# Row softmax on one core: which queue issues the first load, and which load has its last row split

## The chip, the cores and the metric

The kernel runs on one core of a Trainium2 chip. The metric is device time in microseconds (us). Times of several runs are given as their median; the profile is that of one execution.

## What is computed

The input `x` is 16 x 1024 rows of 512 float32 numbers, the output has the same shape:

```python
x_scaled = x / 2.0
x_max = np.max(x_scaled, axis=-1, keepdims=True)
exp_x = np.exp(x_scaled - x_max)
return (exp_x / np.sum(exp_x, axis=-1, keepdims=True)).astype(np.float32)
```

Each row is read once and written once: 33.55 MB in each direction.

## The kernel before, in words

The 16384 rows are 128 rows for each of the 128 partitions. `PLAN` cuts them into ten tiles. Tile 0 has 3 rows a partition, tile 1 has 7, tile 2 has 13, and tiles 3 to 9 have 15 each. Each tile is loaded by one request and stored by one request (with one exception, below), and is worked on in chunks: 1 chunk in tile 0, 2 in tile 1, and 3 in every other tile, of 3 to 5 rows a partition. There are 27 chunks.

All tiles live in one buffer, `arena`, of 98 rows a partition. Tiles 0 to 7 fill it. Tile 8 takes the place of tiles 0 to 2, and tile 9 that of parts of tiles 2 and 3, so their loads have to wait until those tiles are stored (`behind`, `need`). Everything is computed in place.

The engines work on a chunk in this order, with semaphores between them:

- VectorE takes the maximum of each row, negated (`do_max`, L118). The first chunk of a tile waits for the tile's load semaphore `ld[t]`.
- ScalarE computes exp(0.5 x - 0.5 max) row by row, and the same instruction sums the row (L176 for tiles 0 to 5, L211 in a loop for tiles 6 to 9).
- VectorE takes the reciprocal of the sums (L127) and multiplies, in one instruction for a chunk of tiles 1 to 3 (`FUSED`, L131) and row by row elsewhere (L138). It does this two chunks behind the maxima (`LAG` = 2): maximum of chunk k, then reciprocal and product of chunk k - 2.
- SyncE (SP) waits for a tile's last product and issues its store (L158). At the end it waits for the last stores (L162).

Two engines issue loads in `issue_loads`, and each has a DMA queue of its own: SP's is q1 in the profile, ScalarE's is q10. SP issues the load of tile 0 (L105), and later all stores. ScalarE issues all other loads. Tile 1, the tile whose number is `SPREAD`, goes in three requests (L110): its first six rows on all partitions, its last row on partitions 0 to 125, and its last row on partitions 126 and 127. Its first chunk therefore waits for 48 counts of its semaphore instead of 16. The others go whole (L114).

The order in time is written out by hand. `issue_loads(0, 2)` is moved into the program's first block, ahead of the barrier of all engines with which a program starts (L252 and L37 in the profile), so that the loads of tiles 0 and 1 are issued before the engines meet. The loads of tiles 2 to 7 follow behind the barrier, in order, on ScalarE; then ScalarE loads its table of exp (L171). The loads of tiles 8 and 9 stand among its exponentials (L190), behind the last chunk of tiles 4 and 5, each with its wait for the stores that free its place.

Of the kernel before, what the change touches and what calls it, by code (L numbers as in the profile page):

```python
# [14 lines left out]
ARENA = 98  # L15
LAG = 2

SPREAD = 1

AFTER = {8: 4, 9: 5}  # L20

# [7 lines left out]
def kernel(  # L29
# [5 lines left out]
    nc = tc.nc  # L35
# [4 lines left out]
    xf = x.flatten_outer_dims()  # L40
# [24 lines left out]
    def dram(ap, t):  # L65
        b, r, _ = tiles[t]
        return ap[b * P : (b + r) * P].rearrange("(p r) d -> p r d", r=r)

    def sb(t):
        _, r, at = tiles[t]  # L70
        return arena[:, at : at + r, :]
# [9 lines left out]
    ld = [nc.alloc_semaphore(f"ld{t}") for t in range(len(tiles))]  # L81
# [16 lines left out]
    def issue_loads(begin, end):  # L98


        for t in range(begin, end):
            if t in behind:
                continue
            if t == 0:
                nc.sync.dma_start(out=sb(t), in_=dram(xf, t)).then_inc(ld[t], 16)  # L105
            elif t == SPREAD:

                r = tiles[t][1] - 1
                for p, q, lo, hi in ((0, P, 0, r), (0, 126, r, r + 1), (126, P, r, r + 1)):
                    nc.scalar.dma_start(  # L110
                        out=sb(t)[p:q, lo:hi], in_=dram(xf, t)[p:q, lo:hi]
                    ).then_inc(ld[t], 16)
            else:
                nc.scalar.dma_start(out=sb(t), in_=dram(xf, t)).then_inc(ld[t], 16)  # L114

    def do_max(k):
# [5 lines left out]
            negate=True,  # L122
        )._wait_ge(ld[t], 48 if t == SPREAD else 16).then_inc(s_max, 1)

# [102 lines left out]
    entry.instructions = []  # L227
    nc.switch_bb("main", None)
    issue_loads(0, 2)
    first = list(entry.instructions)  # L230
    at = next(k for k, i in enumerate(head) if type(i).__name__ == "InstDrain")
    entry.instructions = head[:at] + first + head[at:]
    act = []
    entry.instructions = list(entry.instructions) + [i for i in jumps if i not in act]
    nc.switch_body(here, parent=None, valid_engines=[i.engine for i in jumps])
    issue_loads(2, len(tiles))
    compute_and_store()

# [29 lines left out]
```

## Time and profile before

| | before |
|---|---|
| median of 10 runs | 160.09 us (160.06 to 160.2) |
| profiled execution, its own time | 160.07 us |
| its span, first to last instruction | 158.7 us |
| busy VectorE, ScalarE | 131.4 us, 94.4 us |
| packets' time on q1 and q10, share of 16 DMA engines | 50.5%, 48.6% |
| first load packet, last store packet's completion | 1.0 us, 158.3 us |
| VectorE's wait for loads | 14.8 us in 5 waits |
| last load landed, last store issued | 127.4 us, 147.2 us |

The span is what the trace covers; the execution's own time has 1.4 us more around it. A page of the profile gives busy times, a strip of 40 slices of the span with the busy share of each engine in tenths, and the DMA queues. "q1" and "q10" are shares of the time of all 16 DMA engines; a tile's load or store is cut into 128 row blocks, one a partition, eight on each engine, and each appears in the trace as a packet with its start, its length and its bytes. Behind the packets of a request, each engine that took part writes a small completion, and these count the semaphore up.

### The profile page before, as it was taken

Reading aid. Unit: us, or ns where it says so; the run is one execution under the profiler, and the core shown is the slowest. Engines: PE = TensorE matmul, PEld = TensorE weight load, DVE = VectorE, ACT = ScalarE, POOL = GpSimd, SP = SyncE. Lnnn points to the kernel's source line nnn. Section 1 sums busy time; section 2 is a strip of 40 time slices with the busy share of each in tenths; the row PEclk is TensorE's granted clock in tenths of the full one; section 3 lists DMA queues with packets and bytes.
Section 4 is the critical chain, followed back from the end, with each engine's and each line's share of the span. In section 5 each row is a group of like instructions: output and inputs, shape, how many; then the busy total and the mean of one; then the engine's idle time right before and its main releaser. Section 6 shows DMA issues by size and latency. Waiting matters only on the chain.

```text
span 158.7 us, 621 instructions
## 1 busy us (share of the span) xinstructions
DVE 131.4 (83%) x155; ACT 94.4 (59%) x257; POOL 0.2 (0%) x4
## 2 busy tenths in 40 slices
DVE  0367699999999999999999999996999379999000
ACT  0359297736964684679638886667566809764000
POOL 0000000000000000000000000000000000000000
DMA  7999999999999999999999999999999999999996
GB/s 262 456 365 429 411 434 460 428 397 436 458 448 401 428 462 451 403 459 403 457 410 457 410 449 418 426 441 418 449 418 449 418 449 418 449 418 441 410 457 263
DMA packets 3026, 67.13 MB, mean 423 GB/s; under 512 B 336, under 2 KB 336, under 8 KB 720
## 3 DMA queue, kind: packets, MB, share of 16 engines
q1 hardware_dynamic: 1584, 34.34, 50.5%
q10 hardware_dynamic: 1440, 32.77, 48.6%
q14 instruction: 2, 0.02, 0.0%
HBM read 33.55 MB, written 33.55 MB: 423 GB/s over the span
## 4 chain that ended last, share of the span: by engine, by line
DMA 52%; DVE 38%; issue 0%
DMA arena<-in_x_dram 38%; DVE stats L118 18%; DMA out_dram<-arena 14%; DVE arena L131 13%; DVE arena L138 7%; DVE recip L127 1%
## 5 line engine op out<-in xcount | busy, mean ns | idle before, releaser
L118 DVE TENSOR_REDUCE stats<-arena 128x5 f32<-128x2560 f32 (+2 forms) x27 | 72.2, 2676 | 14.8 <-DMA arena<-in_x_dram 14.8
L176 ACT ACTIVATE arena<-arena,stats 128x512 f32<-128x512 f32 x68 | 48.2, 710 | 23.7 <-DVE stats L118 23.7
L211 ACT ACTIVATE arena<-arena,stats x60 | 42.5, 710 | 20.5 <-ACTq L203 20.5
L138 DVE TENSOR_SCALAR arena<-arena,recip 128x512 f32<-128x512 f32 x93 | 38.6, 483 | 0.7
L131 DVE TENSOR_TENSOR arena<-arena,recip 128x2560 f32<-128x2560 f32 (+2 forms) x8 | 19.9, 2492 | 0.3
L176 ACT ACTIVATION_READ_ACCUMULATOR arena<-arena,stats 128x1 f32 x68 | 12.7, 187 | 0.0
L211 ACT ACTIVATION_READ_ACCUMULATOR arena<-arena,stats x60 | 11.2, 187 | 0.0
L127 DVE RECIPROCAL recip<-stats 128x5 f32<-128x5 f32 (+2 forms) x27 | 4.8, 178 | 0.0
L171 ACT ACT_TABLE_LOAD x1 | 1.3, 1283 | 5.9 <-issue 5.9
L252 POOL MEMSET const-bfloat16-1.0<- 128x1 bf16 x1 | 0.1, 101 | 0.0
L252 POOL MEMSET const-uint8-127<- 128x1 uint8 x1 | 0.1, 101 | 0.0
L252 POOL MEMSET const-float32-0.0<- 128x1 f32 x1 | 0.1, 98 | 0.2 <-issue 0.2
L252 POOL MEMSET const-float32-1.0<- 128x1 f32 x1 | 0.1, 98 | 0.0
## 6 DMA issues: line engine op xcount, KB each, us to landing
arena<-in_x_dram ACTq DMA_DIRECT2D x7, 3840.0 KB, 46.7
out_dram<-arena SPq DMA_DIRECT2D x7, 3840.0 KB, 22.7
arena<-in_x_dram ACTq DMA_DIRECT2D x1, 3328.0 KB, 14.7
out_dram<-arena SPq DMA_DIRECT2D x1, 3328.0 KB, 20.9
out_dram<-arena SPq DMA_DIRECT2D x1, 1792.0 KB, 17.7
arena<-in_x_dram ACTq DMA_DIRECT2D x1, 1536.0 KB
arena<-in_x_dram SPq DMA_DIRECT2D x1, 768.0 KB, 6.4
out_dram<-arena SPq DMA_DIRECT2D x1, 768.0 KB, 15.7
```

Of the source, the lines that this page charges most:

```text
L118: nc.vector.reduce_max(out=stats[:, b : b + c], in_=arena[:, a : a + c], axis=mybir.AxisListType.X, negate=True,)._wait_ge(ld[t], 48 if t ...
L127: nc.vector.reciprocal(out=recip[:, b : b + c], in_=stats[:, b : b + c])._wait_ge(s_exp, k + 1).then_inc(s_rec, 1)
L131: nc.vector.tensor_mul(out=arena[:, a : a + c], in0=arena[:, a : a + c], in1=recip[:, b : b + c].unsqueeze(2).to_broadcast([P, c, D]),)._w ...
L138: ins = nc.vector.tensor_scalar_mul(out=arena[:, a + r], in0=arena[:, a + r], scalar1=recip[:, b + r : b + r + 1],)
L171: nc.scalar.preload_act_table(mybir.ActivationFunctionType.Exp)
L176: ins = nc.scalar.activation(out=arena[:, a + r], in_=arena[:, a + r], func=mybir.ActivationFunctionType.Exp, bias=stats[:, b + r : b + r ...
L211: ins = nc.scalar.activation(out=data, in_=data, func=mybir.ActivationFunctionType.Exp, bias=stat, scale=0.5, accum_out=stat,)
L252: nc = _bacc.Bacc("TRN2", target_bir_lowering=False, num_devices=1)
```

## The change

`SPREAD` becomes 5, and the branch that gave tile 0 to SP goes:

```diff
-SPREAD = 1
+SPREAD = 5
...
         for t in range(begin, end):
             if t in behind:
                 continue
-            if t == 0:
-                nc.sync.dma_start(out=sb(t), in_=dram(xf, t)).then_inc(ld[t], 16)
-            elif t == SPREAD:
+            if t == SPREAD:
 
                 r = tiles[t][1] - 1
                 for p, q, lo, hi in ((0, P, 0, r), (0, 126, r, r + 1), (126, P, r, r + 1)):
                     nc.scalar.dma_start(
                         out=sb(t)[p:q, lo:hi], in_=dram(xf, t)[p:q, lo:hi]
                     ).then_inc(ld[t], 16)
             else:
                 nc.scalar.dma_start(out=sb(t), in_=dram(xf, t)).then_inc(ld[t], 16)
```

ScalarE now issues tiles 0 and 1, each whole, ahead of the barrier; behind it, it issues tiles 2, 3 and 4 whole, tile 5 in three requests (fourteen rows on all partitions, the last row on partitions 0 to 125, the last row on 126 and 127), and tiles 6 and 7 whole. SP issues stores only. In `do_max`, which is not edited, the count of 48 follows `SPREAD` to tile 5; tile 1's first chunk waits for 16. All shapes of computation, all stores and the loads of tiles 8 and 9 are as before. The line numbers of the profile behind the edit move up by 2.

## The prediction

> **What bounds the kernel now.** I read the page first, then a table by stage, then the DMA view of two stretches at the start, and last the waits.
>
> ```profile
> DVE 131.4 (83%) x155; ACT 94.4 (59%) x257; POOL 0.2 (0%) x4
> ...
> DMA  7999999999999999999999999999999999999996
> ...
> DMA packets 3026, 67.13 MB, mean 423 GB/s; under 512 B 336, under 2 KB 336, under 8 KB 720
> ...
> HBM read 33.55 MB, written 33.55 MB: 423 GB/s over the span
> ```
>
> The DMA line is at 9 in every slice but the first and the last: the 16 DMA engines, not VectorE (83%), are full. Table by stage (stretch, its length, busy DVE, ACT, POOL, clock, DMA share, GB/s):
>
> ```profile
> 0.00:1.00 1.00, 0.00 (x0) 0.00 (x0) 0.20 (x4) 1.00 0.00 0
> 1.00:2.50 1.50, 0.00 (x0) 0.00 (x0) 0.00 (x0) 1.00 0.92 299
> 2.50:6.40 3.90, 0.02 (x1) 0.49 (x1) 0.00 (x0) 1.00 1.03 411
> 6.40:9.70 3.30, 1.76 (x2) 2.33 (x6) 0.00 (x0) 1.00 1.14 407
> ...
> 17.40:59.20 41.80, 41.52 (x25) 27.01 (x75) 0.00 (x0) 1.00 1.01 435
> ...
> 127.90:147.50 19.60, 19.07 (x33) 10.91 (x30) 0.00 (x0) 1.00 1.03 442
> 147.50:157.40 9.90, 0.00 (x0) 0.00 (x0) 0.00 (x0) 1.00 0.96 416
> ```
>
> Nothing moves for 1.0 us; then the engines are full until 157.4, at 299 to 411 GB/s in the first stages and 430 to 442 later. Single packets say the same: the first starts at 1.006 us (SP's load of tile 0, issued at 0.00), a row block of 30720 bytes takes 1.138 us wherever it stands, and the 16 engines write their last completion between 157.43 and 158.26. So the span is first packet + each engine's bytes + what is lost to slow packets, and an edit counts if it changes one of these or lets an engine go empty. VectorE's chain is a second, near bound at the end only: the last load lands at 127.45, VectorE starts on it at 127.85, the last store is issued at 147.17, and its first packet starts at 148.35, directly behind the store before it.
>
> The profiled execution took 160.07 us, 1.37 over its span of 158.7; the median of the ten runs is 160.09. I add differences to 160.09. A measurement of this kernel tells about 0.2% (0.32 us) from no change.
>
> **Part 1: tile 0 moves from SP's queue to the front of ScalarE's.** SP loses one issue of 0.378 us, and nothing else waits there until the first store at 15.04. ScalarE issues tile 0 at L114 where it issued tile 1, at 0.12 us, 0.12 later than SP did. How long ScalarE's first packet takes after its issue is not shown directly:
>
> ```profile
> DMA packets 73, 0.45 MB, mean 179 GB/s; under 512 B 0, under 2 KB 0, under 8 KB 73
> ...
> q1 hardware_dynamic: 73, 0.45, 55.0%
> ```
> ```profile
> q10 hardware_dynamic: 90, 1.11, 81.0%
> q1 hardware_dynamic: 71, 0.34, 23.5%
> ```
>
> The first fence is 0 to 2.5 us, with SP's queue q1 alone; the second 2.5 to 6.0 us, where ScalarE's q10 joins in. Tile 1, issued at 0.12, has its first packet only at 2.52. Is ScalarE's queue late by itself, or had the engines taken SP's packets already? Followed packet by packet, every one of the 16 engines does exactly five packets of q1 (the first 0.23 to 0.73 us, the rest 0.234) before its first of q10, though they began between 1.006 and 1.788 us. One late moment common to all, or one fixed delay, would not give five everywhere: engine by engine they would need windows that don't overlap. So it is a depth to which an engine commits to a queue, and q10's descriptors were there much earlier. The stores show this again: tile 0's store, issued at 15.04, starts at 18.51, behind load packets already taken. Bounds for the shift of the first packet: 0 (issue as early as SP's, same delay of 1.006) to +1.5 (2.52, as if the queue itself were that late). I take ScalarE's 0.12 plus SP's 1.006 = 1.126, a shift of **+0.12 us**, since SP's row is the nearest without another queue ahead. The Trainium skill ("DMA: Bandwidth & Descriptors", "Latency and other measured facts") gives about 0.6 us to the first byte for both issuing engines alike; SP's row has 1.006 - 0.378 = 0.63. By the page ScalarE's first packet would come at 0.12 + 0.385 + 0.6 = 1.1, a shift of 0.1; no row here shows it for ScalarE.
>
> Tiles 0 and 1 no longer share the engines packet by packet. Tile 0 (8 packets an engine, 8 x 0.230 = 1.84 us) lands after about 1.126 + 0.4 (slow first packet) + 1.84 = 3.4 us, on the two engines that start 0.77 later at about 4.2, instead of 6.00. VectorE's first maximum starts near 4.6 instead of 6.38. The 1.8 us are no gain: the next is ScalarE's table load (below) and then tile 1's landing, and the DMA engines stay full throughout.
>
> **Part 2: tile 1 in one piece.** Per engine 8 x 0.531 = 4.25 us, instead of 8 x 0.456 + 9 x 0.080 = 4.37 on fourteen engines and 3.65 on two. Those two are the late starters, 7.84 us at the end of tile 1's wide part against 7.0 to 7.4 for most. Unsplit, all are on tile 2 by about 7.96, where three engines were last at 8.57 to 8.76. Tile 2's last row block ended at 16.91; I expect 16.5, and VectorE's long run from 17.36 starts up to 0.4 earlier. Cost on the end: **0**, as the engines are full and tile 2's store only joins a queue. Without that cover (an engine idle) 0.4 would be a gain, not a loss.
>
> **Part 3: issues around the barrier.** Ahead of the barrier ScalarE issues two DMAs instead of three. Rows of L110: 0.385, 0.665, 0.244. I take 0.385 + 0.5, so L114's later issues begin near 2.2 instead of 2.65 (bounds 2.0 and 2.65). There are then eight issues instead of six: 3.23 + 0.665 + 0.244 = 4.14, ending at 6.3, and the table load of 1.283 ends near 7.6 instead of 7.19. First exponential before: 8.16. So it comes some 0.5 earlier at 7.6, bound by the table load and no longer by VectorE. Tile 2's descriptors come near 3.2 and are needed at 7.1. All of it lies beside full DMA engines: **0**. If that cover were gone, tile 0's store would be late; at 15.04 it has no one waiting for it.
>
> **Part 4: the split in tile 5.** Fourteen engines get 8 packets of 28672 bytes (about 1.06 us each, estimated between the 0.983 of 26624 and 1.134 of 30720 bytes) and nine of 2048 (0.080); two engines get none. Total bytes of every engine are as before, since the row that leaves them sits in another tile: **0** on the last packet. 336 packets under 512 B are 20 x 16 + 14 + 2 completions, and that count stays. What is new is where the small packets run: in tile 1 no other queue was active, while at about 53 us tile 2's store is. There loads and stores alternate one by one in the packets. About four store packets (0.987 each) are left then, so four small loads wait for one each: on most engines tile 5 ends at 53.7 + 0.1 (9 x 0.080 for 8 x 0.074) + 4 x 0.987 = 57.8, and it lands near 58 instead of 55.26. It is wanted by the thirteenth maximum at 64.00: 6 us of cover. Tile 2's store ends 4 us earlier in exchange, then loads run alone until tile 3's store, issued at 59.18 with first packet at 62.73; by then both queues have moved the same bytes as before. The Trainium skill ("DMA: Bandwidth & Descriptors", "Queues, rings and completion order") has an engine drain a packet of typically 9 to 17 descriptors from one ring before it turns to the next. By that the nine small rows would go through together and tile 5 would land near 55.4. The rows contradict it here; both land before 64. If the cover were gone, the maximum would wait 4 us.
>
> **Sum:** +0.12 + 0 + 0 + 0 = +0.12. Slow packets stay, I assume: over their steady lengths they cost, mean per engine, 0.31 us in 1.0 to 2.5, 0.26 in 2.5 to 6.0 and 0.57 in 7.7 to 9.6 (tile 2's first packets take about 1.53 instead of 0.987). I allow -0.06 for less switching between queues. 160.09 + 0.06 = **160.15 us**.
>
> **Rivals.**
>
> *Slower, ScalarE's queue starts late.* For it: the 2.52 above, and no row of ScalarE's queue alone. Against it: five packets everywhere. From 1.39 us for the first packet it adds over 0.32. To have been in turn at the sixth packet, q10 must have been there by the second, at 1.57 at the latest on the engine with the earliest; so the likely price is up to +0.56, 160.65; at 2.52 it is 161.6.
>
> *Slower, the end starves.* The last store is issued at 147.17; with SP's 1.006 it is there at 148.18, and its first packet starts at 148.35: cover of 0.17 us. Tile 9's completions come between 124.76 and 127.44, three engines being one store packet (1.138) behind the others. If the new order puts one more store packet before the last load on the last engine, VectorE ends 1.14 later, and the earlier engines idle for 1.14 - 0.17 = 0.97: from 157.43-157.69 to about 158.4-158.7, over the 158.26 of the latest. Price +0.15 to +0.4: 160.25 to 160.5. Against it: tile 2 lands earlier, and loads run ahead around 60 us.
>
> *Faster, slow packets go.* If the slow stretches after 2.5 us come from two queues or from small rows, 0.26 + 0.57 = 0.83 go: 160.21 - 0.83 = 159.4; the stretch at 7.7 alone: 159.64. Against it: the two engines without small rows are slowed as much (1.53 and 1.57).
>
> *Nothing changes:* the sum, with the shift anywhere near zero.
>
> **Chances.** Forecast 0.45, all within 0.2% (159.77 to 160.41). Late queue 0.25, slower. Starved end 0.12, a third of it within 0.2%. Slow packets gone 0.18, faster. Faster 0.18, same 0.45 + 0.04 = 0.49, slower 0.25 + 0.08 = 0.33. The range is 159.6 to 160.7: below it lies the loss of both slow stretches (about 0.1), above it a queue later than 1.6 us (about 0.1).
>
> **What will show it.** Right: first load packet at 1.1 on q10, no q1 packet before the first store; tile 0's maximum near 4.6, first exponential near 7.6; VectorE's run from about 17.0 to 17.4; tile 5 landing near 58 without an idle VectorE at the thirteenth maximum; last store's first packet directly behind the store before it; last completion near 158.3. Wrong: a first packet after 1.4, an idle gap in q1 near 148, or 430 GB/s already before 9 us.

## The result and the profile after

The changed kernel takes 160.60 us (median of 8 runs, 160.55 to 160.89) against 160.09 (28 runs, 159.98 to 160.23). The ratio is 1.0036, 95% interval 1.0027 to 1.0044: slower by about half a microsecond. The profiled execution took 160.86 us with a span of 159.5, at the upper end of its runs. So the two profiled executions lie 0.79 us apart where the medians lie 0.51 apart, and the details below show more loss than the medians do.

The page of the changed kernel, the lines that answer to those of before:

```profile
DVE 131.5 (82%) x155; ACT 94.3 (59%) x257; POOL 0.2 (0%) x4
...
DMA  6999999999999999999999999999999999989888
...
DMA packets 3026, 67.13 MB, mean 421 GB/s; under 512 B 336, under 2 KB 336, under 8 KB 720
...
HBM read 33.55 MB, written 33.55 MB: 421 GB/s over the span
```

Work, bytes and packets are the same to the unit. New is the end of the DMA strip: 8s where there were 9s. The same table by stage as before (stretch, length, busy DVE, ACT, POOL, clock, DMA share, GB/s):

```profile
1.00:2.50 1.50, 0.00 (x0) 0.00 (x0) 0.00 (x0) 1.00 0.78 242
2.50:6.40 3.90, 1.75 (x1) 0.57 (x1) 0.00 (x0) 1.00 1.05 440
6.40:9.70 3.30, 0.79 (x1) 2.93 (x7) 0.00 (x0) 1.00 1.01 431
...
17.40:59.20 41.80, 41.53 (x25) 27.55 (x76) 0.00 (x0) 1.00 1.00 417
...
127.90:147.50 19.60, 17.65 (x30) 11.18 (x32) 0.00 (x0) 1.00 1.01 433
147.50:157.40 9.90, 1.47 (x4) 0.00 (x0) 0.00 (x0) 1.00 0.94 403
```

From 2.5 to 9.7 us more bytes move than before (440 and 431 GB/s, not 411 and 407). From 17.4 to 59.2 fewer move at about the same DMA share: 417, not 435. The table counts a packet whole in the stretch in which it starts, which is why a share can be over 1; with each packet counted only as far as it lies in the stretch, the two rates are 421 and 431. The engines are busy and slower. The start, in the timeline of the changed kernel (start, length, engine, line, operation):

```profile
4.61 1.75 DVE L116 TENSOR_REDUCE stats<-arena 128x3 f32<-128x1536 f32 x1 [4.61 <-DMA arena<-in_x_dram]
...
5.83 1.28 ACT L169 ACT_TABLE_LOAD   x1 [5.83 <-issue]
...
7.12 0.72 ACT L174 ACTIVATE arena<-arena,stats 128x512 f32<-128x512 f32 x1
...
16.82 2.82 DVE L116 TENSOR_REDUCE stats<-arena 128x5 f32<-128x2560 f32 x1 [2.57 <-DMA arena<-in_x_dram]
```

VectorE's long run starts at 16.82, not 17.36. At the other end its first maxima of tiles 8 and 9, in the kernel before and then in the changed one:

```profile
109.69 2.82 DVE L118 TENSOR_REDUCE stats<-arena 128x5 f32<-128x2560 f32 x1 [1.24 <-DMA arena<-in_x_dram]
...
127.85 2.82 DVE L118 TENSOR_REDUCE stats<-arena 128x5 f32<-128x2560 f32 x1 [3.28 <-DMA arena<-in_x_dram]
```
```profile
111.50 2.82 DVE L116 TENSOR_REDUCE stats<-arena 128x5 f32<-128x2560 f32 x1 [3.27 <-DMA arena<-in_x_dram]
...
129.67 2.82 DVE L116 TENSOR_REDUCE stats<-arena 128x5 f32<-128x2560 f32 x1 [3.29 <-DMA arena<-in_x_dram]
```

Both come 1.8 us later. VectorE waits longer for tile 8 (3.27 us, not 1.24) and as long as before for tile 9. The last store is issued at 149.0 instead of 147.2, and DMA engines go idle ahead of the last two stores. Two stretches there, in the kernel before and then in the changed one:

```profile
139.50:141.00 1.50, 1.46 (x3) 0.21 (x3) 0.00 (x0) 1.00 0.95 410
149.00:150.50 1.50, 0.00 (x0) 0.00 (x0) 0.00 (x0) 1.00 0.95 410
```
```profile
139.50:141.00 1.50, 1.50 (x2) 1.50 (x5) 0.00 (x0) 1.00 0.82 348
149.00:150.50 1.50, 0.00 (x0) 0.00 (x0) 0.00 (x0) 1.00 0.77 328
```

Such short stretches are coarse beside packets of 1.1 us. Followed packet by packet, the engines stand idle for 0.53 us each on average ahead of the last two stores of the changed kernel, and for 0.00 in the kernel before.

So three things are late at once: the first packet (1.157 us, not 1.006), packets in the middle that take longer than their usual time, and a starved end. The obvious story is the last, the rival named in the prediction. The experiments are about whether it is the true one.

A measure used below is the **slow-packet time**: each packet's length over the steady length of its size (1.138 us for 30720 bytes), summed and divided by 16 engines. Up to 130 us it is 1.34 us in the profile before and 1.68 after.

### The profile page after: what moved, and what is told of

It is laid out like the page before. It is cut to its first block, busy times and chain, and to the rows that moved or that the text cites. A ratio compares the mean times of both kernels' runs of the same rounds, so it can differ in the third digit from the quotient of the medians.

```text
span 159.5 us, 621 instructions
## 1 busy us (share of the span) xinstructions
DVE 131.5 (82%) x155; ACT 94.3 (59%) x257; POOL 0.2 (0%) x4
## 4 chain that ended last, share of the span: by engine, by line
DMA 54%; DVE 38%; issue 0%
DMA arena<-in_x_dram 39%; DVE stats L116 18%; DMA out_dram<-arena 15%; DVE arena L129 13%; DVE arena L136 6%; DVE recip L125 1%
## 5 line engine op out<-in xcount | busy, mean ns | idle before, releaser
L116 DVE TENSOR_REDUCE stats<-arena 128x5 f32<-128x2560 f32 (+2 forms) x27 | 72.2, 2676 | 16.5 <-DMA arena<-in_x_dram 16.5
```

The lines of the kernel that those rows point to most:

```text
L116: nc.vector.reduce_max(out=stats[:, b : b + c], in_=arena[:, a : a + c], axis=mybir.AxisListType.X, negate=True,)._wait_ge(ld[t], 48 if t ...
```

## The experiments

First the two halves of the change apart, and a variant without any split.

**e1: only tile 0 on ScalarE's queue**

```diff
 # of the changed kernel
-SPREAD = 5
+SPREAD = 1
```

> Only one half of the change: tile 0 on ScalarE's queue, the split row still in tile 1. Theory A (the small packets of tile 5, beside tile 2's store, let the stores get ahead, so tile 9's load lands at 129.2 instead of 127.4 and the end starves): without them tile 9 lands at 127.3 to 127.9, no gap in SP's queue between the last three stores, 160.1 to 160.3 us. Theory B (VectorE's run starts at 16.8 instead of 17.4, so every store comes 0.5 earlier beside loads that come no earlier): if that run starts before 17.1 here, tile 9 lands after 128.5 and the time is 160.4 to 160.7; if it starts at 17.3 or later, 160.1 to 160.3. Theory C (only ScalarE's later first packet counts): 160.2 to 160.3 in any case.

Measured: 160.28 us, ratio 1.0008 (0.9999 to 1.0017). VectorE's run started at 17.08, tile 9's load landed at 127.9, no idle engine before the end. That is what theory A expected; theory C gave about the time too. Theory B, with a run that starts before 17.1, had tile 9 after 128.5.

**e2: only the split in tile 5, tile 0 on SP**

```diff
 # of the kernel before
-SPREAD = 1
+SPREAD = 5
```

> The other half: tile 0 on SP's queue as before, the split row in tile 5. Theory A: small packets beside tile 2's store, tile 9 lands at 128.5 to 129.2, gaps of 0.3 to 0.8 us in SP's queue ahead of the last two stores, 160.4 to 160.6 us. Theory B: decided by the start of VectorE's run: 17.2 or later gives 160.0 to 160.2, before 17.0 gives 160.4 or more. Theory C: first packet at 1.0 again, 160.0 to 160.1.

Measured: 160.62 us, ratio 1.0032 (1.0020 to 1.0043). Tile 9 landed at 129.0, and the strip ends as in the changed kernel:

```profile
DMA  7999999999999999999999999999999999989888
```

With tile 0 on SP the move of the split gives as much loss as the whole change. Theory C falls: the first packet was at 1.02.

**e3 and e4: no split, tile 0 on ScalarE's queue (e3) or on SP's (e4)**

```diff
 # of the changed kernel (e3), of the kernel before (e4)
-SPREAD = 5        # e4: 1
+SPREAD = None
```

> Tile 0 on ScalarE's queue, and no tile split. Every engine moves the same bytes, so the two engines that start late keep 0.72 us that the split took from them. Theory A: no small packets at all, tile 9 lands at 127.3 to 127.9 and the stores follow without gaps; the end is set by the two late engines, 160.2 to 160.7. Theory B: VectorE's run starts at 16.8 as in the changed kernel, tile 9 lands at 129 and the last stores come after gaps, 160.5 to 160.7. The landing of tile 9 and the gaps tell the two apart, not the time.

> Tile 0 on SP's queue, no tile split: the fourth corner beside tile 0 on ScalarE's queue without a split (160.37). First packet at 1.0. Theory A (small packets beside tile 2's store make the end starve): no small packets, tile 9 lands by 128.0, no gaps in SP's queue ahead of the last two stores, 160.0 to 160.3 us, with the end set by engines that start late and are not relieved. If ScalarE's later start is worth what its first packet says, this is 0.15 us under the kernel with tile 0 on ScalarE's queue and no split.

Measured: e3 160.37 us, ratio 1.0021 (1.0012 to 1.0030); e4 160.11, ratio 1.0000 (0.9991 to 1.0009). In e3 VectorE's run started at 16.69, earlier than in the changed kernel, and yet tile 9 landed at 127.9 without a gap: theory B falls. So it is the split in tile 5 that costs, not the missing split in tile 1: e4 has neither and is as fast as the kernel before, whose split relieves two engines (160.09).

**e5: the starved end undone**

```diff
 # of the changed kernel
-            nc.sync.wait_ge(s_mul, last_chunk[t] + 1)
+            nc.sync.wait_ge(s_mul, last_chunk[t] + (2 if t == 4 else 1))
```

> The changed kernel, in which tile 4's store waits for one chunk more (issued near 78.4 instead of 73.4), so that SP's queue runs empty for a while near 80 us and loads take its turns. If the loss is a starved end (theories A and B): one or two store packets fewer go ahead of the last load, tile 9 lands at 127 to 128.2, the gaps ahead of the last two stores shrink to under 0.2 us, 160.1 to 160.4 us. If the loss is elsewhere (slow packets between 16 and 60 us, the first packet): no change of the time beyond 0.1 us, 160.5 to 160.7.

Measured: the landing and the gaps moved as expected: tile 9 at 127.0, last store issued at 146.7, and the two stretches are full:

```profile
139.50:141.00 1.50, 1.47 (x4) 0.56 (x1) 0.00 (x0) 1.00 1.15 492
149.00:150.50 1.50, 0.00 (x0) 0.00 (x0) 0.00 (x0) 1.00 0.90 389
```

But the time did not: 160.54 us, ratio 1.0031 (1.0019 to 1.0043), as the second branch had it. This is the first doubt about the obvious story.

**e7: small packets on all sixteen engines**

```diff
 # of the changed kernel
-    ... in ((0, P, 0, r), (0, 126, r, r + 1), (126, P, r, r + 1)):
+    ... in ((0, P, 0, r), (0, P, r, r + 1)):
...
-        )._wait_ge(ld[t], 48 if t == SPREAD else 16).then_inc(s_max, 1)
+        )._wait_ge(ld[t], 32 if t == SPREAD else 16).then_inc(s_max, 1)
```

> The changed kernel with tile 5's last row as one request over all 128 partitions: small packets on all sixteen engines, none relieved. Theory A: small packets beside tile 2's store are enough; the latest engine again lets one store packet more ahead of the last load, tile 9 lands after 128.5, gaps ahead of the last two stores, 160.5 to 160.8 us. Rival: the imbalance counts (two engines without small packets, which keep alternating while the others empty SP's queue): tile 9 lands by 128.0, no gaps, 160.2 to 160.5.

Measured: 161.06 us, ratio 1.0055 (1.0041 to 1.0069), tile 9 landing at 129.0, small gaps. Small packets in tile 5 are enough to make tile 9 late; the rival of the imbalance falls. The time is above both expectations: here, as far as the packets can be followed engine by engine, the two engines that start late also end late (last completions at 158.80 on average, 159.61 on the latest).

**e8: the split in tile 7, where stores are always waiting**

```diff
 # of the changed kernel
-SPREAD = 5
+SPREAD = 7
```

> All loads on ScalarE's queue, the split in tile 7, where SP's queue has stores waiting all the time. If loads and stores take turns one by one, however small the load: eight or nine of the small packets wait for a store packet of 1.138 us each, tile 7 lands 8 to 10 us later than in the changed kernel (92.9), near 102; VectorE stands still for 6 to 9 us before tile 7's first maximum; 161.8 to 164 us. If an engine takes several small packets in one turn: tile 7 lands before 95, 160.3 to 160.8 us.

Measured: 164.95 us, ratio 1.0304 (1.0288 to 1.0319), above the 161.8 to 164 of the first branch; tile 7 landed at 103.8. VectorE in the timeline of this kernel:

```profile
104.18 2.82 DVE L116 TENSOR_REDUCE stats<-arena 128x5 f32<-128x2560 f32 x1 [11.14 <-DMA arena<-in_x_dram]
```

It stands still for 11.14 us at tile 7's first maximum, more than the 6 to 9 expected. 103.8 less the changed kernel's 92.9 is 10.9, between nine and ten store packets of 1.138. In the packets' records a small packet and a store packet alternate on almost every engine that has small ones. Loads and stores take turns one by one, and 2 KB wait as long for their turn as 30 KB.

**e9 and e13: the split in tile 2 or tile 4, tile 0 on SP**

```diff
 # of the kernel before
-SPREAD = 1
+SPREAD = 2        # e13: 4
```

> Tile 0 on SP's queue, the split in tile 2: small packets at about 16 us, before the first store's packets. Theory A: no store beside them, so nothing gets ahead; tile 9 lands by 128.0, no gaps, 160.0 to 160.3 us. If small packets cost as such, wherever they stand after tile 1: 160.4 to 160.6.

> Tile 0 on SP's queue, the split in tile 4: small packets near 40 us, beside the last one or two packets of tile 1's store, at a place where SP's queue runs empty at 42 to 43 us in any case. With the split in tile 5 that queue runs empty once more, near 57.5 us instead of staying full, and tile 6's first packets are slow there (0.21 to 0.30 us an engine between 57 and 62 us, against 0.00 without). If the loss of the place comes from that emptied queue: 0.00 between 57 and 62 us here, tile 9 landing by 128, 160.0 to 160.25 us. If small packets beside a store cost as such: 0.2 more than with no split between 42 and 49 us, 160.3 to 160.6.

Measured: e9 160.14 us, ratio 1.0001 (0.9992 to 1.0010), tile 9 at 127.6. e13 160.43 us, ratio 1.0022 (1.0013 to 1.0031), tile 9 at 128.9, with gaps. In e13 the slow packets moved with the split: none between 57 and 62 us, but 0.28 us an engine at 40 to 41.5, where fourteen of sixteen engines had a slow first packet of tile 5. They came earlier than the stretch that the second expectation named, and its time was met. Of the first expectation only the 0.00 between 57 and 62 us came; the landing and the time did not.

**e10, e11 and e12: is the starved end the price?** Only the first row of each chunk of tiles 8 and 9 is multiplied, in the changed kernel (e10) and in the kernel before (e11), so that their stores are issued early; e12 is the changed kernel again, beside them.

```diff
-        for r in range(c):
+        for r in range(c if t < 8 else 1):
```

> The changed kernel; of tiles 8 and 9 only the first row of each chunk is multiplied, the other products are left out. All transfers and their order up to tile 9's landing stay, but the last two stores are issued some 3 to 5 us earlier, so no engine can run dry. What the time falls by, against the changed kernel beside it, is what the starved end costs net: 0.4 to 0.5 us (160.1 to 160.2) if it is nearly the whole loss; about 0.2 (160.35 to 160.5) if slow packets and the late start make up the rest, as the packets' records add up (idle time of 0.6 us an engine, of which 0.4 only evens out engines that would end at different times); 0 (160.6) if it is none of it.

> The kernel before, with the same products of tiles 8 and 9 left out. If its end is set by full DMA engines, as read from its profile, with a cover of 0.17 us ahead of the last store, nothing changes: 160.0 to 160.2. If VectorE's last products still set the end there, it falls by 0.2 or more, under 159.9.

> The changed kernel itself, as the measure for the kernel with the products left out, on the same chip: 160.5 to 160.7 us, tile 9 landing at 129, last store issued near 149.

Measured: e10 160.60 us, ratio 1.0032 (1.0020 to 1.0044); e12 160.63, ratio 1.0035 (1.0021 to 1.0049); e11 160.07, ratio 1.0002 (0.9993 to 1.0011). In e10 tile 9 landed at 129.1 as late as in e12, but the last store was issued at 144.2, and no engine stands idle ahead of the last two stores:

```profile
139.50:141.00 1.50, 0.88 (x3) 1.50 (x5) 0.00 (x0) 1.00 0.91 389
149.00:150.50 1.50, 0.00 (x0) 0.00 (x0) 0.00 (x0) 1.00 1.14 492
```

The idle time is gone and 0.03 us is gained, far inside the intervals. The executions of e10 and of e12 each scatter by about 0.26 us, so a price of up to about 0.2 us is not excluded (an estimate from that scatter); half of the loss or more is. In the changed kernel the starved end is real and costs little. That answers with the third branch of the expectation, "none of it", or close to it. Why it can: without the gaps the engines end apart (e10: 158.34 on average, 158.92 the latest), with them together (changed kernel: 159.04 and 159.13). The average engine gains 0.70 us, the latest one 0.21, and these two profiled executions differ by 0.08 (160.78 and 160.86). Idle time is spent mostly by engines that would have been early.

**What the packets' records add up to**, one profile of each kernel, slow-packet time an engine in us; in brackets tile 0's queue and the split tile:

| kernel | time | first packet, mean of 16 | 0.9-7 | 7-10 | 10-20 | 20-57 | 57-62 | sum to 130 |
|---|---|---|---|---|---|---|---|---|
| before (SP, 1) | 160.09 | 1.25 | 0.57 | 0.57 | 0.03 | 0.12 | 0.00 | 1.34 |
| e11 (SP, 1, fewer products) | 160.07 | 1.19 | 0.54 | 0.43 | 0.04 | 0.33 | 0.00 | 1.37 |
| e9 (SP, 2) | 160.14 | 1.31 | 0.41 | 0.00 | 0.45 | 0.31 | 0.00 | 1.22 |
| e4 (SP, none) | 160.11 | 1.19 | 0.49 | 0.00 | 0.10 | 0.55 | 0.00 | 1.19 |
| e13 (SP, 4) | 160.43 | 1.20 | 0.42 | 0.00 | 0.38 | 0.67 | 0.00 | 1.53 |
| e2 (SP, 5) | 160.62 | 1.19 | 0.55 | 0.00 | 0.21 | 0.68 | 0.21 | 1.70 |
| e1 (ScalarE, 1) | 160.28 | 1.33 | 0.50 | 0.42 | 0.03 | 0.44 | 0.00 | 1.41 |
| e3 (ScalarE, none) | 160.37 | 1.37 | 0.49 | 0.01 | 0.28 | 0.70 | 0.00 | 1.51 |
| changed (ScalarE, 5) | 160.60 | 1.43 | 0.41 | 0.01 | 0.29 | 0.65 | 0.25 | 1.68 |
| e12 (the same) | 160.63 | 1.29 | 0.45 | 0.02 | 0.30 | 0.87 | 0.23 | 1.93 |
| e10 (the same, fewer products) | 160.60 | 1.35 | 0.45 | 0.01 | 0.27 | 0.74 | 0.24 | 1.76 |
| e5 (the same, store held) | 160.54 | 1.36 | 0.48 | 0.03 | 0.25 | 0.64 | 0.16 | 1.61 |
| e7 (ScalarE, 5, all engines) | 161.06 | 1.36 | 0.38 | 0.03 | 0.28 | 0.86 | 0.30 | 1.90 |

The sums are lowest where the time is (1.19 to 1.37 at 160.07 to 160.14) and highest where it is longest (1.68 to 1.93 from 160.60 up). The split in tile 5 puts 0.16 to 0.30 us between 57 and 62, behind its small packets; every kernel without it has 0.00 there. With the split in tile 1 a stretch of 0.42 to 0.57 lies behind the small packets too, but then 10 to 20 us is almost free (0.03 to 0.04), where the others have 0.10 to 0.45. Kernel e8 is left out: there the engines stand idle for 4.9 us each.

In eight of these kernels no engine stands idle at the end: before, e11, e9, e4, e1, e3, e5 and e10. There the columns "first packet" and "sum" added together go with the time: 2.38 to 2.59 us at 160.07 to 160.14, 2.74 and 2.88 (e1, e3) at 160.28 and 160.37, 2.97 and 3.11 (e5, e10) at 160.54 and 160.60. The pair e11 and e10, the kernel before and the changed one with the same products left out, differs by 0.16 in the first packet and 0.39 in the slow packets, 0.55 together, beside 0.53 in the medians. The gaps' price is open where tile 0 is on SP: e13 and e2, with gaps, take 0.15 and 0.25 us longer than e1 and e3, whose two columns come to the same.

This is bookkeeping over one profile a kernel, and the changed kernel alone gave 1.68 and 1.93 in two profiles, so small differences between rows say little. With it goes the way in which slow packets move with the split (e9, e13). No run took them away alone.

## Why the prediction was right or wrong

**What bounds the kernel: right.** Full DMA engines, not VectorE: e11 leaves out most of the last products and stays at 160.07.

**Part 1, tile 0 on ScalarE's queue: right in kind, a little small.** The first packet came at 1.157 us, against 1.126; the queue's own delay is 1.157 - 0.124 = 1.03, as SP's, and the rival of a late queue (160.65) fell. The five packets were rightly read as no lateness of ScalarE's queue, but they are no fixed depth: in e4, also with tile 0 on SP, 39 of SP's packets on the 16 engines had begun before ScalarE's first, at 1.95 us, where the kernel before had 74, at 2.52. Alone the move is not clear of zero with the split in tile 1 (e1), and e3 over e4 is 160.37 - 160.11 = 0.26. The estimate was 0.12.

**Part 2: right.** Tile 2's last row block ended at 16.46 (16.5 expected), and VectorE's run began 0.54 us earlier, a little more than the 0.4 allowed. At the end it is worth nothing: e4, this part alone, takes 160.11.

**Part 3: right.** The issues took less than worked out; the table load ended at 7.11 and the first exponential came at 7.12, against 7.6. That this is worth nothing at the end was not tested apart.

**Part 4: right on the cover, wrong on the sum.** Tile 5 landed at 58.6 (58 worked out) and VectorE waited for nothing there; it took the thirteenth maximum at 63.46. The turn-taking by which 58 was worked out is what e8 shows. But the step "0 on the last packet", because every engine's bytes stay, failed: e2, which is Parts 2 and 4 together, takes 0.5 us longer than e4, which is Part 2 alone.

**The sum is where it failed**, in the words "Slow packets stay, I assume", with -0.06 for less switching. They did not stay. The stretch at 7.7 to 9.6 went (0.57 to 0.01), as the faster rival said. But more came back later: 0.29 against 0.03 before 20 us, 0.65 against 0.12 to 57, and 0.25 behind the small packets. Net it is +0.34 in the first pair of profiles, where -0.06 was put down, a term for which no row was given and no run shows anything. With the first packet's +0.15 that makes 0.49. That it is so near to the 0.51 between the medians is partly chance, since these two executions lie 0.79 apart and the changed one has idle engines too; the pair e11 and e10, without idle engines, is the better one (0.55 beside 0.53). Such a sum of averages explains the size, and does not prove it. A sign stood in the profile before: the prediction read that a row block of 30720 bytes takes 1.138 us wherever it stands, while 16 such load packets between 29 and 49 us took 1.166 to 1.494.

**The starved end happened, at a lower price.** Three conditions of that rival came true: one more store packet ahead of the last load on the latest engines, tile 9 1.73 us later, idle engines. Its price of 0.15 to 0.4 us is not what e10 shows: 0.03, with up to about 0.2 not excluded. A reader of the changed profile alone, me included, would have named it as the cause.

Of the prediction's three signs of being wrong two came: the idle gap in q1, near 150 us, and 440 GB/s before 9 us. So the range holds 160.60, but the likeliest case, "within 0.2%", was not the one that came; it is the slower side, which had 0.33, and by a mechanism that no rival described: slow packets that move instead of staying or going. The range reached as far as 160.7 for the sake of a late queue, which did not come; that it holds the time is luck.

**Open:** what makes a load's packets slow. They come where many engines begin a new load together, up to about 60 us; in later loads single ones at most. Tile 8's load in e8, begun behind the same small packets near 101 us, had none. Address, time and alignment of the engines were not told apart. A hint for alignment stands at the changed kernel's end: behind the first gap, 15 engines begin a store packet between 141.62 and 141.79 us and take 1.156 to 1.178 for it, and of the 391 packets of 30720 bytes after 130 us only 148 take the usual 1.138; in e10, without gaps, 377 of 391 do. Also open is why ScalarE's queue costs less beside the split in tile 5 (changed kernel over e2: nothing) than without a split (0.26).

## What to carry to other kernels

Where the DMA engines are full, equal bytes on every engine are not equal time: compare the length of single packets before and after, stage by stage, and not only shares. Idle time at the end of a stream is worth only what the latest engine gains from its removal, so take the cause away (here by leaving out work behind it) before naming it the price. And put small packets where no other queue is active, since each of them waits for a whole packet of the other queue.

## What the runs showed of the hardware

- In the kernel before, all sixteen engines had taken five packets from SP's queue before ScalarE's came to its turn; in e4 it was about three (39 packets in all at ScalarE's first, against 74). From then on the two queues alternate packet by packet, whatever the sizes. In e8 nine small packets cost tile 7 10.9 us. The Trainium skill ("DMA: Bandwidth & Descriptors", "Queues, rings and completion order") has an engine drain typically 9 to 17 descriptors of one ring before it switches; the measurement decides here: a turn was one row block, of 2048 bytes as of 30720.
- The first packet follows the start of its issue by 1.01 us on SP (kernel before) and 1.03 on ScalarE (changed kernel); behind the end of the issue it is 0.63 and 0.65.
- The 126 and 2 split relieves two engines. Beside e7, the same split over all engines, it is worth 161.06 - 160.60 = 0.46 us in tile 5, and nothing in tile 1 (160.09 before, 160.11 in e4, without a split).
- The first packets of a load that many engines begin together run longer than later ones of the same size: 1.53 us instead of 0.987 for tile 2's in the kernel before, 0.12 to 0.87 us an engine between 20 and 57 us. What makes them long stays open.
